# The planner of a 2-layer encoder kernel is given other durations for TensorE's products, and a price for each change of tile form

## The chip, the cores and the metric

One core of a Trainium2 chip. The metric is the device time of one launch in microseconds (us); lower is better. The kernel before took 1587.9 us (median of 3 runs, 1582.06 to 1589.01).

## The reference, cut to what matters

The kernel computes a small transformer-like trunk: one sequence of 256 tokens, width 1024, two layers, all in float32.

```python
for l in range(DEPTH):                       # 2
    h = modulate(rmsnorm(x, norm_gains[l, 0]), sh1, sc1)
    x = x + 0.5 * gt1 * swiglu(h, ffn_wi[l, 0], ffn_wo[l, 0])      # 1024 -> 2 x 2816 -> 1024
    h = modulate(rmsnorm(x, norm_gains[l, 1]), sh2, sc2)
    x = x + gt2 * hybrid_mixer(h, ...)
    h = modulate(rmsnorm(x, norm_gains[l, 2]), sh3, sc3)
    x = x + 0.5 * gt3 * swiglu(h, ffn_wi[l, 1], ffn_wo[l, 1])
return rmsnorm(x, final_norm)

# hybrid_mixer: proj = h @ w_in, then three token mixers of 8 heads x 64, then
merged = (sigmoid(gz0) * (o_a @ w_branch[0])      # a: dilated window attention
          + sigmoid(gz1) * (o_b @ w_branch[1])    # b: neighbourhood attention on a grid
          + sigmoid(gz2) * (o_c @ w_branch[2]))   # c: RWKV-7 recurrence, forward and backward
return merged @ w_out
```

The shifts, scales and gates (sh1, sc1, gt1 and so on) come from a conditioning vector through the weights `ada_w`.

## The kernel before, in words

**Dense work.** Activations lie transposed, features on the partitions and the 256 tokens along the free dimension. Every float32 weight tile is split in two parts, `whi` (ScalarE, line 352) and `wlo` (VectorE, line 361), each activation likewise, and one dense step is three matmuls of 128x128 by 256 (lines 395 to 398). Weights stream from HBM: SP issues a load of 512 KB (line 337), ScalarE and VectorE split it in quarters of 512 columns, and each quarter serves four dense steps. The product of the attention's v uses steps of three matmuls of 512 columns (lines 1645 to 1647). `pearly` are dense products that start before the norm is known.

**Mixer.** Its dense work is the stream of projections, gates and branch products in the order "cabAgB" (line 27): the recurrence's inputs first, then both attentions' inputs, then gates and branches a and b, and last the branch of the recurrence, whose input is `oC`. Beside it runs *thin* work: many small products on 64x64, 64x128, 128x64 or 128x32 parts of TensorE's array. The recurrence is computed in 4 chunks of 64 tokens in each of two directions. `invert` (line 1142) builds the chunk's matrix (pG), inverts its 8x8 blocks (p from m and b8), and doubles the block size three times (pX, pT); `values` prepares pBT, pvt, pMV; `scan` (line 1275) goes from chunk to chunk (pAS, pU, pS1, pY); `post` (line 1373) normalises the result (pvar, a square root, pgi) and writes `oC`. `attend` (line 1465) does the attentions (pS, pPT, po). Each of these steps has VectorE or ScalarE work between its products.

**The order.** Every engine runs its instructions in the order in which they were issued, and that order is made by a planner, `Order` (lines 58 to 155), when the program is built. The work is written as threads (generators). A thread asks for an engine and a duration with `on(engine, duration)` before it issues the instructions; `od.run` always lets that thread go on whose request can start earliest in planned time, and of several the one of the lowest priority number. The dense stream (`main`, line 1783) has priority 7, so thin work that is ready goes first; the splitting of weights has -1. A planned result can be used after a latency (line 36: 0.2 us after TensorE, 0.15 after ScalarE, 0.13 after VectorE). One rule speaks for the dense stream: thin work adds up in `thin`, and once that is over 2.25 us the dense stream goes first until it has had two steps in a row (lines 122 and 139 to 146). `clock` (line 103) slows planned products where TensorE has been little used. The planned durations decide the order and nothing else: no instruction waits for a planned time. The loads of `ada_w` are requested at planned times (`ada`, line 492: every 5 us in the first feed-forward part, every 7 us from 110 us after the start of the mixer).

A dense step is planned at `MM`, 0.329 us. A form of products (64x64 and so on) is not known to the planner before.

```python
36  LAT, MM = {"PE": 0.2, "ACT": 0.15, "DVE": 0.13, "SP": 0.0}, 0.329
...
139                 if a == "PE":
140                     if th is self.dense:
141                         self.row += 1
142                         if self.row >= BURST:
143                             self.thin = 0.0
144                     else:
145                         self.row = 0
146                         self.thin += b
147                     b = self.clock(t, b, 0.98 if th is self.dense else 0.6) - t
148                 self.free[a] = t + b
149                 th.t = t + b + lat
```

Of the kernel before, what the change touches and what calls it, by code (L numbers as in the profile page):

```python
# [34 lines left out]
WPRIO = -1  # L35
LAT, MM = {"PE": 0.2, "ACT": 0.15, "DVE": 0.13, "SP": 0.0}, 0.329
VPRIO = 4
# [20 lines left out]
class Order:  # L58
# [6 lines left out]
    def __init__(self):  # L65
        self.threads, self.free, self.cur, self.n = [], {}, None, 0
        self.dense, self.cols, self.thin, self.row, self.tab = None, {}, 0.0, 0, None

    def spawn(self, gen, prio, dense=False):
# [47 lines left out]
    def run(self):  # L117
        while self.threads:
# [11 lines left out]
            if kind == "on":  # L130
# [5 lines left out]
                if a == "ACT" and th.req[4] not in (None, self.tab):  # L136
                    self.tab = th.req[4]
                    b += 1.28
                if a == "PE":
                    if th is self.dense:  # L140
                        self.row += 1
                        if self.row >= BURST:
                            self.thin = 0.0
                    else:
                        self.row = 0
                        self.thin += b
                    b = self.clock(t, b, 0.98 if th is self.dense else 0.6) - t
# [10 lines left out]

def on(eng, dur, lat=None, tab=None):
    return ("on", eng, dur, LAT[eng if isinstance(eng, str) else eng[0]] if lat is None else lat, tab)  # L160

# [26 lines left out]
def trunk(ctx, tc, A, out):  # L188
# [404 lines left out]
    def rstd(st):  # L593
# [3 lines left out]
        p = paux("pss")  # L597
        yield on("PE", 0.6)
        for t in range(2):
# [268 lines left out]
    def mixer(l, st):  # L868
# [92 lines left out]
        def lowrank(d, q, tw, xl_, lw, pe):  # L961
# [37 lines left out]
            p = paux("pa", (128, 2, S))  # L999
            yield on("PE", 0.86)  # L1000
            for h in range(2):
# [12 lines left out]
        def kk_norm():  # L1014

            pss = None
            for d in range(2):
                yield wait(e_rkv[d, 1])
                yield take(s_big)
                kq = big("kq")  # L1020
                for hp in range(4):
                    yield on("ACT", 0.4)
                    S_.activation(kq[:, hp], RKV[d, 1][:, hp], AF.Square, scale=vec[:, 6, hp:hp + 1])
                if d == 0:
                    yield take(s_px)
                    pss = paux("pkk", (128, S))
                yield on("PE", 0.5)
                head_sum(pss, d, kq, d == 1)
                free_big()
# [17 lines left out]
        def finish():  # L1047
            pbs = None
            for d in range(2):
                yield wait(e_rkv[d, 0])  # L1050
                yield wait(e_kk)
                for q in range(2):
# [8 lines left out]
                    p = paux("pinv", (128, 2, S))  # L1061
                    yield on("PE", 0.434)
                    head_bcast(p, d, q, KK)
# [37 lines left out]
                if d == 0:  # L1101
                    yield take(s_px)
                    pbs = paux("pbs", (128, S))
                yield on("PE", 0.5)
                head_sum(pbs, d, RKV[d, 1], d == 1)
# [7 lines left out]
            for d in range(2):  # L1113
                yield wait(e_rkv[d, 2])
                v = RKV[d, 2]
                for q in range(2):
                    sl = slice(2 * q, 2 * q + 2)
                    yield take(s_px)
                    p = paux("pbon", (128, 2, S))
                    yield on("PE", 0.434)  # L1120
                    head_bcast(p, d, q, rows)
# [20 lines left out]
        def invert(d, cc):  # L1142
            for c in cc:
# [10 lines left out]
                for i in range(4):  # L1154
                    yield on("PE", 0.435, 0.2 if i == 3 else 0.0)
                    for b in range(2):
# [12 lines left out]
                for lv in range(3):  # L1169
                    by = lambda t: t.rearrange("p h (q a s) -> p h q a s", a=2, s=8 << lv)  # L1170
                    yield take(s_px)
                    px = paux("pX", (128, 4, 64))
                    yield on("PE", 0.615)
                    for h in range(8):
# [8 lines left out]
                    pt = paux("pT", (128, 4, 64))  # L1183
                    yield on("PE", 0.615)
                    for h in range(8):
# [54 lines left out]
        def values(d, c, G, bu, W1, cs_, done):  # L1240
            yield wait(e_rkv[d, 2])
            v = RKV[d, 2]
            for b in range(2):
                hs = half(b)
                yield take(s_px)
                p = paux("pBT", (128, 4, 64))
                yield on("PE", 0.22)
                for i in range(4):
# [5 lines left out]
            p = paux("pvt", (128, 4, 64))  # L1254
            yield on("PE", 0.648)
            for h in range(8):
# [6 lines left out]
            p = paux("pMV", (128, 4, 64))  # L1263
            yield on("PE", 0.615)
            for h in range(8):
# [9 lines left out]
        def scan(d):  # L1275
            ST = None
            order = list(range(4)) if d == 0 else [3, 2, 1, 0]
            for n, c in enumerate(order):
# [4 lines left out]
                if ST is not None:  # L1283
                    yield take(s_px)
                    p = paux("pAS", (128, 4, 64))
                    yield on("PE", 0.615)
                    for h in range(8):
# [5 lines left out]
                p = paux("pU", (128, 4, 64))  # L1293
                yield on("PE", 0.615)
                for h in range(8):
# [7 lines left out]
                if n < 3:  # L1303
                    yield take(s_px)
                    p = paux("pS1", (128, 4, 64))
                    yield on("PE", 0.615)
                    for h in range(8):
# [13 lines left out]
                p = paux("pY", (128, 4, 64))  # L1321
                yield on("PE", 1.275 if ST is not None else 0.615)
                for h in range(8):
# [49 lines left out]
        def post(d, t):  # L1373
# [13 lines left out]
            p = paux("pvar", (128, 8))  # L1387
            yield on("PE", 0.8)
            for hp in range(4):
# [75 lines left out]
        def attend(br, hps, qT, kT, vv, evs, o, pp, done):  # L1465
# [6 lines left out]
            for hp in hps:  # L1472
# [11 lines left out]
                pS = [paux("pS", (128, 2, S)) for _ in range(2)]  # L1484
                yield on("PE", 0.96)
                for t in range(2):
# [37 lines left out]
                po = paux("po", (128, S))  # L1524
                yield on("PE", 0.96)
                for j in range(2):
# [100 lines left out]
        def qkv(br):  # L1627
# [11 lines left out]
            for kk in range(KT):  # L1639
                yield from tl.whole()  # L1640
                wh, wl = tl.last
                for t in range(2):
                    xs = slice(t * 128, (t + 1) * 128)
                    yield on("PE", 0.65, 0.0)
                    P.matmul(p[t], ha.hi(kk)[:, xs], wh, start=kk == 0, stop=False)  # L1645
                    P.matmul(p[t], ha.hi(kk)[:, xs], wl, start=False, stop=False)
                    P.matmul(p[t], ha.lo(kk)[:, xs], wh, start=False, stop=kk == 7)  # L1647
# [260 lines left out]
```

## Time and profile before

| what | before |
|---|---|
| median of 3 runs | 1587.9 us |
| lowest, highest run | 1582.06, 1589.01 us |
| the profiled execution's own time | 1586.35 us |
| its span, first to last instruction | 1584.6 us |
| mean granted TensorE clock | 0.985 of full speed |
| TensorE busy | 1533.1 us, 97% |
| VectorE busy | 1311.7 us, 83% |
| ScalarE busy | 897.0 us, 57% |
| matmul records | 14518 |

The profile is of one execution. PE is TensorE, DVE VectorE, ACT ScalarE; PEclk is the clock that was granted to TensorE, as a share of full speed. The start of a matmul is measured and its end is modelled: matmuls overlap in the records, so the distance from one start to the next tells what one costs, and a busy engine can still have short waits in it. One float32 matmul of a thin product stands as two records, so a product of eight has 16.

### The profile page before, as it was taken

What the parts mean: (1) busy time and instruction counts of PE and PEld (TensorE: products, weight loads), DVE (VectorE), ACT (ScalarE), POOL (GpSimd) and SP (SyncE); (2) the same over time, 40 slices, a digit from 0 to 9 for tenths busy, and PEclk for the clock granted to TensorE, in tenths of its full rate; (3) what the DMA queues carried; (4) which work ended last, traced back from release to release, by engine and by line L of the source; (5) the groups of instructions that cost most, each with busy time, mean ns of one, the idle gap of its engine ahead of it and who ended that gap; (6) DMA issues with size and microseconds to landing.
All of it is one profiled execution on the core that took longest, in us unless ns stands there. A gap on an engine that the chain in (4) does not pass through costs nothing.

```text
span 1584.6 us, 36797 instructions
## 1 busy us (share of the span) xinstructions
PE 1533.1 (97%) x14518; PEld 1450.6 (92%) x14518; DVE 1311.7 (83%) x2938; ACT 897.0 (57%) x1854; POOL 21.3 (1%) x29
## 2 busy tenths in 40 slices
PE   3999999999999989999999999999999999999998
PEld 3999999988888889999999999998888987999997
DVE  7878889989888869997779877898888896888664
ACT  4655567576554447554565545676655445565554
POOL 3100000000000000000000000000000000000000
PEclk7999999999999989999999999999999999899999
DMA  8588864545464225888657876544446422467553
GB/s 310 188 293 272 284 230 163 180 130 198 140 230 140 74 80 174 277 287 273 226 200 272 285 266 203 185 159 155 160 159 232 168 102 68 136 202 274 184 184 127
DMA packets 91621, 311.61 MB, mean 197 GB/s; under 512 B 11444, under 2 KB 14772, under 8 KB 91448
## 3 DMA queue, kind: packets, MB, share of 16 engines
q1 hardware_dynamic: 91160, 309.15, 57.8%
q8 instruction: 114, 1.87, 0.5%
q14 instruction: 59, 0.48, 0.1%
q10 hardware_dynamic: 288, 0.10, 0.0%
HBM read 308.17 MB, written 1.05 MB: 195 GB/s over the span
## 4 chain that ended last, share of the span: by engine, by line
PE 88%; DMA 5%; DVE 4%; issue 1%; ACT 1%; SPq 0%; DVEq 0%; ACTq 0%
PE pmain L396 21%; PE pmain L397 20%; PE pmain L398 20%; DMA araw<-in_ada_w_dram 5%; PE pearly L396 2%; PE pearly L398 2%; PE pearly L397 2%; PE pX L1175 2%; PE pT L1186 2%; PE pG L1158 1%; PE pS L1488 1%; PE po L1528 1%; DVE wlo L361 1%; PE pmain L1645 1%; PE pmain L1647 1%
## 5 line engine op out<-in xcount | busy, mean ns | idle before, releaser
L352 ACT CAST whi<-wraw 128x512 fp32r<-128x512 f32 x836 | 511.9, 619 | 427.3 <-PE pmain L397 256.0
L361 DVE TENSOR_TENSOR wlo<-wraw,whi 128x512 fp32r<-128x512 f32 x836 | 571.7, 688 | 118.7 <-ACT whi L352 109.2
L396 PE MATMUL pmain<-h,whi 128*128 128x256 f32 x1872 | 539.2, 288 | 0.0
L398 PE MATMUL pmain<-h,wlo 128*128 128x256 f32 x1872 | 525.2, 281 | 1.1 <-DVE wlo L361 1.1
L397 PE MATMUL pmain<-h,whi 128*128 128x256 f32 x1872 | 525.2, 281 | 0.0
L396 PEld LDWEIGHTS pmain<-h,whi 128*128 128x128 f32 x1872 | 351.7, 188 | 13.3 <-issue 4.6
L398 PEld LDWEIGHTS pmain<-h,wlo 128*128 128x128 f32 x1872 | 352.2, 188 | 1.6 <-DVE wlo L361 1.6
L397 PEld LDWEIGHTS pmain<-h,whi 128*128 128x128 f32 x1872 | 352.3, 188 | 0.4
L460 DVE CUSTOM_DVE_ANT_0 araw<-araw,csb 128x1024 f32<-128x1024 f32 x137 | 169.0, 1235 | 47.6 <-DMA araw<-in_ada_w_dram 47.2
L398 PE MATMUL pmain<-z,wlo 128*128 128x256 f32 x704 | 198.2, 282 | 3.4 <-DVE wlo L361 3.3
L397 PE MATMUL pmain<-z,whi 128*128 128x256 f32 x704 | 197.9, 281 | 0.0
L396 PE MATMUL pmain<-z,whi 128*128 128x256 f32 x704 | 197.8, 281 | 0.0
L398 PEld LDWEIGHTS pmain<-z,wlo 128*128 128x128 f32 x704 | 132.6, 188 | 4.4 <-DVE wlo L361 4.2
L396 PEld LDWEIGHTS pmain<-z,whi 128*128 128x128 f32 x704 | 132.6, 188 | 0.0
L397 PEld LDWEIGHTS pmain<-z,whi 128*128 128x128 f32 x704 | 132.6, 188 | 0.0
L396 PE MATMUL pearly<-xh,whi 128*128 128x258 f32 x320 | 91.4, 286 | 0.0
L398 PE MATMUL pearly<-xh,wlo 128*128 128x258 f32 x320 | 90.4, 282 | 0.0
L397 PE MATMUL pearly<-xl,whi 128*128 128x258 f32 x320 | 90.2, 282 | 0.0
L397 PEld LDWEIGHTS pearly<-xl,whi 128*128 128x128 f32 x320 | 60.6, 189 | 0.0
L396 PEld LDWEIGHTS pearly<-xh,whi 128*128 128x128 f32 x320 | 60.4, 189 | 0.0
L398 PEld LDWEIGHTS pearly<-xh,wlo 128*128 128x128 f32 x320 | 60.3, 189 | 0.0
L419 ACT CAST z<-ffz 128x256 fp32r<-128x256 f32 x76 | 30.7, 405 | 40.3 <-DVE ffz L651 39.9
(306 smaller groups left out, 2459.2 us busy)
## 6 DMA issues: line engine op xcount, KB each, us to landing
wraw<-in_ffn_wi_dram SPq DMA_DIRECT2D x164, 512.0 KB, 4.9
araw<-in_ada_w_dram SPq DMA_DIRECT2D x137, 512.0 KB, 6.4
wraw<-in_ffn_wo_dram SPq DMA_DIRECT2D x88, 512.0 KB, 4.5
wraw<-in_w_in_dram SPq DMA_DIRECT2D x78, 512.0 KB, 3.7
wraw<-in_w_gb_dram SPq DMA_DIRECT2D x72, 512.0 KB, 4.2
wraw<-in_w_out_dram SPq DMA_DIRECT2D x16, 512.0 KB, 3.6
w0raw<-in_ffn_wi_dram SPq DMA_DIRECT2D x12, 512.0 KB, 9.8
raw<-in_ada_w_dram SPq DMA_DIRECT2D x7, 512.0 KB, 7.9
```

Source lines behind the costliest of these rows:

```text
L352: S_.copy(hi, part(q))
L361: V.tensor_tensor(lo, part(q), hi, op=OP.subtract)
L396: P.matmul(o, w[0], xh, start=first, stop=False)
L397: P.matmul(o, w[0], xl, start=False, stop=False)
L398: P.matmul(o, w[1], xh, start=False, stop=last)
L419: S_.copy(self.hi(k), src)
L460: V.tensor_tensor_reduce(out=raw, in0=raw, in1=csb, scale=0.5, scalar=0.0, op0=OP.mult, op1=OP.add, accum_out=modT[l][:, blk:blk + 1])
L1158: P.matmul(pp[b][:, i], BK[d][i // 2][hs, i % 2, c].rearrange("p a b -> p (a b)"), ar_view(d, i // 2)[hs, :, i % 2, cs_], start=True, stop ...
L1175: P.matmul(px[half(h), h // 2], G[half(h), h // 2, h % 2, 0:64], T[half(h), h // 2], start=True, stop=True)
L1186: P.matmul(pt[half(h), h // 2], X[half(h), h // 2], TT[half(h), h // 2], start=True, stop=True)
L1488: P.matmul(pS[e][:, t], qT[half(e), hp, t * 128:(t + 1) * 128], kT[half(e), hp], start=True, stop=True)
L1528: P.matmul(po[half(e)], vv[:, j, (2 * hp + e) * 64:(2 * hp + e + 1) * 64], pt_[:, 2 * e + j], start=j == 0, stop=j == 1)
```

## The change

No instruction is added or removed. The planner gets other durations for TensorE's requests: a dense step 0.354 (was 0.329), a step of the v product 0.7 (0.65), eight 64x64 products 0.48 (0.615), each of the four requests of pG 0.22 (0.435), and so on. Each request on TensorE can now name its form; one that names none is of the full array (or of the 65 rows of pwz). Where the form differs from that of the request planned before it on TensorE, 0.2 us (`TURN`) is added, and this sum also goes into `thin`. All other code is as before. The sites that are alike stand once, with their number.

```diff
-LAT, MM = {"PE": 0.2, "ACT": 0.15, "DVE": 0.13, "SP": 0.0}, 0.329
+LAT, MM = {"PE": 0.2, "ACT": 0.15, "DVE": 0.13, "SP": 0.0}, 0.354
+TURN = 0.2
...
+        self.form = None
...
                 if a == "PE":
+                    if th.req[5] != self.form:
+                        self.form = th.req[5]
+                        b += TURN
                     if th is self.dense:
...
-def on(eng, dur, lat=None, tab=None):
-    return ("on", eng, dur, LAT[eng if isinstance(eng, str) else eng[0]] if lat is None else lat, tab)
+def on(eng, dur, lat=None, tab=None, form=None):
+
+    return ("on", eng, dur, LAT[eng if isinstance(eng, str) else eng[0]] if lat is None else lat, tab, form)
...
         p = paux("pss")
-        yield on("PE", 0.6)
+        yield on("PE", 0.9)
...
             p = paux("pa", (128, 2, S))
-            yield on("PE", 0.86)
+            yield on("PE", 0.86, form="64x128")
...
                     pss = paux("pkk", (128, S))
-                yield on("PE", 0.5)
+                yield on("PE", 0.44, form="128x32")
...
                     p = paux("pinv", (128, 2, S))
-                    yield on("PE", 0.434)
+                    yield on("PE", 0.48, form="64x128")
...
                 for i in range(4):
-                    yield on("PE", 0.435, 0.2 if i == 3 else 0.0)
+                    yield on("PE", 0.22, 0.2 if i == 3 else 0.0, form="64x128")
...
                     px = paux("pX", (128, 4, 64))
-                    yield on("PE", 0.615)
+                    yield on("PE", 0.48, form="64x64")
...
                 p = paux("pBT", (128, 4, 64))
-                yield on("PE", 0.22)
+                yield on("PE", 0.25, form="64x128")
...
                     p = paux("pS1", (128, 4, 64))
-                    yield on("PE", 0.615)
+                    yield on("PE", 0.48, form="128x64")
...
                 p = paux("pY", (128, 4, 64))
-                yield on("PE", 1.275 if ST is not None else 0.615)
+                yield on("PE", 1.05 if ST is not None else 0.48, form="128x64")
...
             p = paux("pvar", (128, 8))
-            yield on("PE", 0.8)
+            yield on("PE", 0.9)
...
                 pS = [paux("pS", (128, 2, S)) for _ in range(2)]
-                yield on("PE", 0.96)
+                yield on("PE", 0.87, form="64x128")
...
                 po = paux("po", (128, S))
-                yield on("PE", 0.96)
+                yield on("PE", 0.87, form="128x64")
...
                 for t in range(2):
                     xs = slice(t * 128, (t + 1) * 128)
-                    yield on("PE", 0.65, 0.0)
+                    yield on("PE", 0.7, 0.0)
```

pX's edit stands for pT, pMV, pAS and pU (0.615 to 0.48) and pvt (0.648 to 0.48), all of form 64x64; pkk's for pbs; pinv's for pbon. pwz, pcum, pPT, p, pg and pgi keep their durations and name no form.

## Rows read from the trace of the kernel before

**Rows 1.** The page: busy time of the engines, and the chain by engine.

```profile
PE 1533.1 (97%) x14518; PEld 1450.6 (92%) x14518; DVE 1311.7 (83%) x2938; ACT 897.0 (57%) x1854; POOL 21.3 (1%) x29
...
PE 88%; DMA 5%; DVE 4%; issue 1%; ACT 1%; SPq 0%; DVEq 0%; ACTq 0%
```

**Rows 2.** Stretches: length, busy us and count of each engine, granted clock, DMA.

```profile
core 0: us, PE busy (x) PEld busy (x) DVE busy (x) ACT busy (x) POOL busy (x), PEclk, DMA share, GB/s
100.00:200.00 100.00, 98.86 (x833) 98.31 (x832) 84.99 (x170) 53.53 (x104) 1.07 (x9) 1.00 0.84 286
600.00:700.00 100.00, 100.00 (x851) 100.00 (x850) 91.24 (x196) 62.16 (x124) 0.00 (x0) 1.00 0.72 247
...
300.00:569.00 269.00, 266.23 (x3111) 230.68 (x3109) 229.19 (x601) 147.65 (x345) 0.00 (x0) 1.00 0.45 149
1072.00:1341.00 269.00, 266.28 (x3111) 230.79 (x3109) 229.09 (x602) 147.71 (x344) 0.00 (x0) 1.00 0.44 149
...
500.00:569.00 69.00, 68.93 (x1160) 59.63 (x1154) 54.69 (x160) 31.18 (x66) 0.00 (x0) 1.00 0.23 78
569.00:577.60 8.60, 3.78 (x45) 2.95 (x44) 5.04 (x12) 4.63 (x10) 0.00 (x0) 0.78 0.19 61
577.60:584.20 6.60, 6.56 (x28) 6.14 (x29) 3.78 (x9) 2.03 (x4) 0.00 (x0) 0.51 0.00 0
...
1349.30:1355.80 6.50, 6.40 (x28) 5.97 (x29) 3.62 (x9) 1.91 (x5) 0.00 (x0) 0.53 0.00 0
```

**Rows 3.** Timeline of VectorE at 602 us: a wlo and its successor.

```profile
602.24 0.69 DVE L361 TENSOR_TENSOR wlo<-wraw,whi 128x512 fp32r<-128x512 f32 x1
602.84 0.48 DVE L535 SCALAR_TENSOR_TENSOR xl<-xT,Ac,xh 128x256 fp32r<-128x256 f32 x1
```

**Rows 4.** Timeline of TensorE, 551.8 to 556 us: start, duration, what.

```profile
551.80 0.68 PE L1288 MATMUL pAS<-ST,ar 64*64 64x64 f32 x16
552.41 0.39 PE L396 MATMUL pmain<-o,whi 128*128 128x256 f32 x1
...
552.96 0.68 PE L1175 MATMUL pX<-txw,G 64*64 64x64 f32 x16
553.58 0.46 PE L1249 MATMUL pBT<-c_ident,bk 64*128 64x64 f32 x4
553.97 0.68 PE L1296 MATMUL pU<-txw 64*64 64x64 f32 x16
554.48 0.63 PE L1186 MATMUL pT<-txw 64*64 64x64 f32 x16
555.04 0.39 PE L396 MATMUL pmain<-o,whi 128*128 128x256 f32 x1
...
555.95 0.45 PE L1324 MATMUL pY<-G,bu 128*64 128x64 f32 x8
```

**Rows 5.** Timeline of TensorE: the first change of form in layer 0.

```profile
261.97 1.03 PE L972 MATMUL pwz<-lw,xlow 65*128 65x256 f32 x4
```

**Rows 6.** Timeline of TensorE, 568.8 to 578 us.

```profile
568.79 0.28 PE L398 MATMUL pmain<-o,wlo 128*128 128x256 f32 x1
569.00 0.33 PE L1324 MATMUL pY<-G,bu 128*64 128x64 f32 x2
570.05 0.68 PE L1324 MATMUL pY<-G,bu 128*64 128x64 f32 x14 [0.72 <-ACT bu L1300]
...
572.47 1.05 PE L1390 MATMUL pvar<-c_sel,gsq 128*128 128x2 f32 x8 [1.13 <-ACT gsq L1382]
575.12 1.11 PE L1408 MATMUL pgi<-c_ident,gsq 128*128 128x128 f32 x4 [1.59 <-DVE gsq L1403]
577.64 0.58 PE L396 MATMUL pmain<-oC,whi 128*128 128x256 f32 x1 [1.41 <-ACT oC L1435]
```

**Rows 7.** Stretches, with line 396 alone: its count is that of dense steps.

```profile
300.00:450.00 150.00, 58.37 (x196) 36.86 (x196) 1.00 0.52 172
450.00:500.00 50.00, 20.98 (x67) 12.57 (x67) 1.00 0.52 180
500.00:569.00 69.00, 18.93 (x57) 10.69 (x57) 1.00 0.23 78
```

**Rows 8.** Waits of TensorE: for whom, us in total, times, longest.

```profile
PE pmain L398 <- DVE wlo L361: 4.4, 5, 1.6
...
PE p L1222 <- DVE m L1217: 3.7, 4, 1.0
...
PE pX L1175 <- DVE txw L1238: 1.4, 2, 0.8
```

More of the change, by code (lines that the diff above doesn't have):

```diff
@@ L1103, in finish @@
                     pbs = paux("pbs", (128, S))
-                yield on("PE", 0.5)
+                yield on("PE", 0.44, form="128x32")
                 head_sum(pbs, d, RKV[d, 1], d == 1)
@@ L1119, in finish @@
                     p = paux("pbon", (128, 2, S))
-                    yield on("PE", 0.434)
+                    yield on("PE", 0.48, form="64x128")
                     head_bcast(p, d, q, rows)
@@ L1183, in invert @@
                     pt = paux("pT", (128, 4, 64))
-                    yield on("PE", 0.615)
+                    yield on("PE", 0.48, form="64x64")
                     for h in range(8):
@@ L1254, in values @@
             p = paux("pvt", (128, 4, 64))
-            yield on("PE", 0.648)
+            yield on("PE", 0.48, form="64x64")
             for h in range(8):
@@ L1263, in values @@
             p = paux("pMV", (128, 4, 64))
-            yield on("PE", 0.615)
+            yield on("PE", 0.48, form="64x64")
             for h in range(8):
@@ L1285, in scan @@
                     p = paux("pAS", (128, 4, 64))
-                    yield on("PE", 0.615)
+                    yield on("PE", 0.48, form="64x64")
                     for h in range(8):
@@ L1293, in scan @@
                 p = paux("pU", (128, 4, 64))
-                yield on("PE", 0.615)
+                yield on("PE", 0.48, form="64x64")
                 for h in range(8):
@@ L1305, in scan @@
                     p = paux("pS1", (128, 4, 64))
-                    yield on("PE", 0.615)
+                    yield on("PE", 0.48, form="128x64")
                     for h in range(8):
```

## The prediction, made before the change was run

> **What bounds the kernel now.** I read the page's busy times first, then its chain, then stretches, then the waits. TensorE is busy 97% of the span, and the chain that ends last runs through it for 88% [rows 1]. So time is what TensorE does, plus the few places where it stands still or runs at the lower clock. The stretches show where those are [rows 2]. In the dense stage from 600 to 700 us it is busy 100.00 of 100 us at a granted clock of 1.00, the 2.4 GHz level. In the mixer's two stretches of mixed work, 300 to 569 and 1072 to 1341 us, it is busy 266.2 and 266.3 of 269. Right behind each comes a hole: 3.78 us busy of 8.60, then a stretch at 0.51 of the clock, the 1.2 GHz level with an edge at each end; layer 1 repeats it. The chip granted less after TensorE had been mostly idle.
>
> The change alters no instruction, only the order in which a planner written in Python issues them. So three things can move: the holes, the number of times TensorE changes its tile form, and the stalls of an engine that meets an instruction too early. The profiled execution took 1586.35 us for a span of 1584.6; the median of the three runs is 1587.9, 1.5 us above it, which I treat as nothing.
>
> **How wrong the plan is before.** VectorE's costs in the plan are right: a wlo starts 0.60 us before its successor [rows 3] and is planned at 0.6. TensorE's are too low. From 600 to 700 us 851 dense products run, 283.7 steps of three; planned at 0.329 that is 93.3 us of the 100, at 0.354 it is 100.4 [rows 2]. In mixed work I take one piece, from the pAS at 551.80 to the pY at 555.95, 4.15 us [rows 4]. Before: 0.615 (pAS) + 0.329 + 0.615 (pX) + 0.22 (pBT) + 0.615 (pU) + 0.615 (pT) + 2 x 0.329 = 3.67. After, with 0.2 at each change of form: 0.68 + 0.554 + 0.68 + 0.45 + 0.68 + 0.48 + 0.908 = 4.43. So the plan goes from 12% fast to 7% slow here. The same reckoning over all 3111 products from 300 to 569 us [rows 2] gives 242.6 us before and 275.8 after, against 269.
>
> **What a change of form costs.** A thin product and one dense step, 551.80 to 552.96, take 1.16 us [rows 4]; the plan's own 0.48 and 0.354 leave 0.33 for two changes, about 0.16 each. There are 223 a layer, from the pwz at 261.97 [rows 5] to the pvar at 572.47 [rows 6], 446 in all and some 70 us. A visit to dense work in between costs two, 0.32 us.
>
> **The sum, part by part.** The work itself: same products, 0.
>
> The holes. In layer 0 the last dense product before the hole starts at 568.79 and oC's first one at 577.64 [rows 6]: the chain of the last chunk (pY, ACT's square, pvar, a square root, pgi, VectorE's products, the cast of oC) is run with nothing beside it. TensorE's stands in 569.0 to 577.6 are 8.60 - 3.78 = 4.8 us, and by pitch rather than by modelled ends some 5.9 (8.7 us less pY 1.2, pvar 1.0, pgi 0.6). Then 577.6 to 584.2 holds 28 products, 6.6 us at half clock, worth 3.3 [rows 2]. Together 9.1 us a layer, 18.2 for both. What would fill it is dense work left over when the recurrence ends. Why more is left: the recurrence waits on VectorE and ScalarE, whose planned times stay; a dense step now fills 0.354 of such a wait and not 0.329, and 0.554 where it follows a thin product. Bounds: from 300 to 569 us there are 196 + 67 + 57 = 320 dense steps [rows 7]. Replaying the planner's rule for bursts (lines 139 to 147) over that order, 54 of them are forced by the sum of thin work; the other 266 fill waits (the v product's steps are left aside). At least 0.025/0.354 = 7% of these, 19 steps or 6.7 us, come free if the waits set the pace, and none if thin work does. At most, if the recurrence took its old 242.6 planned us, 1 - 242.6/275.8 = 12% of 269, 32 us, come free. I take the lower figure that has waits in it, 6.7 us: over the 5.9 idle, and with the idle gone I let the stretch at half clock go too. So -18.2, between 0 and -18.2, since no hole is left after that.
>
> The stalls. Before, the plan was 10% fast on TensorE, so operands were there when it came. That slack goes. Its idle time in mixed work is now 269 - 266.2 and 269 - 266.3, 5.5 us in both layers [rows 2]; most of it is p behind m, 3.7, and pX, 1.4 [rows 8]. I let it double, as the smallest step that a lost slack of 10% suggests: +5.5, between 0 and +13.6 (worked out with the second rival).
>
> The other edits. pG's four planned steps of 0.435 become four of 0.22, so fewer bursts cut it up and a few changes of form may go. pss, pvar, pkk, pbs, pinv and pbon occur at most 8 times a layer. The v product's 0.70 for 0.65 follows the same ratio as the dense step. All 0, covered by the chain of waits around them, at worst a microsecond or two.
>
> The loads of the modulation weights are issued at planned times (every 5 or 7 us); with a plan no longer 10% fast they come some 8 to 10% closer in real time, on SP's queue ahead of weight loads. DMA is at a share of 0.84 from 100 to 200 us [rows 2], and TensorE's waits for wlo are 4.4 us in all [rows 8]. Between 0 and another 4.4; I take +1, nearer to nothing, since those waits are five in some 1000 us of dense work.
>
> Sum: 1586.35 - 18.2 + 5.5 + 1 = 1574.7, so **1575**.
>
> **Rivals.** First, thin work sets the pace and the holes stay. In the last 69 us 26 of 57 dense steps [rows 7] are forced, and the budget that forces them fills as before: thin work planned at 44.8 us then is 35.4 plus 48 entries of 0.2, 45.0. For it: TensorE is at 68.93 of 69 there [rows 2]. Against: before 500 us only 28 steps are forced, against the 196 + 67 that run there [rows 7], and the recurrence is on its way from some 360 us on. Time 1586.
>
> Second, slower: the stalls. A change is priced 0.2 and costs 0.16, so the plan is now slow in mixed work, 275.8 against 269. Products are put where the plan has their operands ready, and TensorE, in order, gets there early. It can lose at most what the plan is too slow, 6.8 us a layer, 13.6 in all; it decides if most of the 85 dense visits a layer end at an operand that comes within the 0.08 us (two changes of 0.04) by which a visit is over-priced. Holes unfilled: 1586.4 + 13.6 = 1600, half of it 1593. Against: VectorE is busy 229 of 269 us [rows 2], and has queued work rather than late work.
>
> Third, more changes of form. A visit of two steps can become one of one step, since one now fills 0.554 planned us. If 44 such visits are added, 44 x 0.32 = 14 us, 1600 with the holes as they are. The Trainium skill (TensorEngine Tiling, Key Properties) says that a change of tiling mode drains the engine, so that their number counts and not only their length; the 0.16 us here agrees.
>
> Fourth, the other way: chains ripen together during longer planned visits, and a tenth to a fifth of the 446 changes go, 7 to 14 us at 0.16. Beside filled holes: 1561 to 1568, about 1565.
>
> **How the numbers follow.** Forecast 0.45, holes stay 0.22, stalls 0.13, more changes 0.05, fewer changes 0.15. Faster or slower begins at 0.5%, 8 us (under 1580, over 1596), about what a measurement can tell. Faster: most of the forecast, 0.38, and 0.14 of the last, 0.52. Slower: 0.17 from stalls, more changes and holes that stay with new stalls. Same: 0.31. The range reaches from the fourth rival nearly in full, 1562, to the second and third nearly in full, 1598.
>
> **What would show it.** Dense products beside the last pY, pvar and pgi of each layer, and a granted clock of 1.00 through that stretch; if pgi still has an idle microsecond ahead of it, the filling was wrong. Changes of form near 446; p, pX or pY with more idle time before them than now would show the stalls. The dense stages should keep their length. I would be wrong if the mixed stretch itself grew while the holes closed: then work only moved.

## The result: slower by 1.4%, though the holes closed

The changed kernel takes 1607.88 us, the median of four runs from 1602.44 to 1612.11. Before it was 1584.98, the median of four. The ratio is 1.0142, with a 95% interval of 1.0114 to 1.0171. The forecast was 1575 with a range up to 1598, so the result lies outside on the slow side. The profiled execution of after took 1610.05 us for a span of 1607.9, that of before 1586.35 for 1584.6: +23.3 us of span to explain. In after the lines of the kernel file that are named here have a number higher by 6 (L361 is L367, L460 is L466).

The page of after, busy time and chain by engine, to be held against [rows 1], with one group of VectorE's instructions, its reductions:

```profile
PE 1539.5 (96%) x14518; PEld 1453.3 (90%) x14518; DVE 1315.4 (82%) x2963; ACT 893.6 (56%) x1833; POOL 21.5 (1%) x29
...
PE 71%; DVE 14%; DMA 10%; issue 3%; ACT 1%; SPq 0%; DVEq 0%; ACTq 0%
...
L466 DVE CUSTOM_DVE_ANT_0 araw<-araw,csb 128x1024 f32<-128x1024 f32 x137 | 169.0, 1235 | 74.9 <-DMA araw<-in_ada_w_dram 74.8
```

The same 14518 products run, but the chain now leaves TensorE for 29% of the span where it left it for 12%: VectorE went from 4% to 14%, DMA from 5% to 10%. The last line says what they do there. L466 is the reduction that VectorE makes of each block of modulation weights, `araw`. It idled 74.8 us ahead of these for their DMA, 46 times; before it was 47.2 us, 39 times. The waits of VectorE (for whom, us in total, times, longest), before:

```profile
DVE araw L460 <- DMA araw<-in_ada_w_dram: 47.2, 39, 3.2
```

After:

```profile
DVE araw L466 <- DMA araw<-in_ada_w_dram: 74.8, 46, 4.7
```

Then the stretches of after, columns as in [rows 2]: one whole stage of up products in layer 0 (the second feed-forward), the last 9.20 us ahead of oC's products in layer 0, where the hole was, and one piece inside that up stage.

```profile
core 0: us, PE busy (x) PEld busy (x) DVE busy (x) ACT busy (x) POOL busy (x), PEclk, DMA share, GB/s
643.43:754.75 111.32, 106.84 (x866) 105.82 (x865) 92.26 (x185) 55.66 (x111) 0.00 (x0) 0.97 0.79 269
576.00:585.20 9.20, 9.20 (x82) 9.20 (x81) 7.13 (x14) 5.16 (x11) 0.00 (x0) 1.00 0.67 209
743.60:747.00 3.40, 3.40 (x17) 3.40 (x17) 3.37 (x7) 0.93 (x2) 0.00 (x0) 0.50 0.66 187
```

And the same up stage before:

```profile
639.02:740.53 101.51, 101.51 (x866) 101.51 (x865) 90.49 (x185) 55.30 (x111) 0.00 (x0) 1.00 0.82 284
```

The hole is gone: where [rows 2] had 3.78 us busy of 8.60 and then a stretch at 0.51 of the clock, TensorE is now busy 9.20 of 9.20 us at 1.00; over the whole chain from the last pY to oC, 565.00 to 585.22, it is busy 20.22 of 20.22. But a stage with the same 866 products takes 111.32 us for 101.51, with 4.5 us of idle time and a mean clock of 0.97. Seventeen products fill 3.40 us at a clock of 0.50, the 1.2 GHz level, in the middle of dense work.

Cut at the first product of each stage, TensorE's timeline gives the whole account:

| stretch, us | before | after | |
|---|---|---|---|
| seven feed-forward stages with modulation loads | 590.4 | 614.9 | +24.5 |
| mixed stage, layer 0 / 1 | 329.1 / 329.1 | 328.9 / 334.5 | +5.3 |
| oC stage behind it, layer 0 / 1 | 14.8 / 14.5 | 11.3 / 11.4 | -6.6 |
| all other | 306.7 | 306.9 | +0.2 |

Of the 24.5, stops account for 16.6 by TensorE's pitch: 20 gaps of over 0.3 us between two products' starts, 22.1 us beyond the usual 0.118, where before there were 6 with 5.5. The lower clock accounts for 5.1, half of 10.2 us in three stretches. The remaining 2.8 is pitch, the distance from one start to the next where nothing stops.

Last, TensorE's waits in after, against [rows 8] (for whom, us in total, times, longest):

```profile
PE pmain L404 <- DVE wlo L367: 18.7, 17, 2.0
...
PE p L1228 <- DVE m L1223: 6.4, 11, 1.5
...
PE pX L1181 <- DVE txw L1244: 5.3, 12, 1.2
```

The wait for `wlo`, 4.4 us before, is 18.7: a product waits for the low half of a weight that VectorE has not split yet. VectorE's busy time has not grown (1311.7 to 1315.4). So VectorE has the time, and does the split late.

**One stop, followed.** Timelines of after show why (start, duration, what, and in brackets the idle time ahead of it with what ended that). SP's queue:

```profile
732.11 2.31 SPq L343 DMA_DIRECT2D wraw<-in_ffn_wi_dram  x2
734.47 0.44 SPq L493 DMA_DIRECT2D araw<-in_ada_w_dram  x1
```

VectorE in the same stretch:

```profile
733.37 0.69 DVE L367 TENSOR_TENSOR wlo<-wraw,whi 128x512 fp32r<-128x512 f32 x1
734.91 1.22 DVE L466 CUSTOM_DVE_ANT_0 araw<-araw,csb 128x1024 f32<-128x1024 f32 x1 [0.85 <-DMA araw<-in_ada_w_dram]
736.07 0.08 DVE L466 DVE_READ_ACCUMULATOR2_ANT modT<- 128x1 f32 x1
736.07 1.29 DVE L367 TENSOR_TENSOR wlo<-wraw,whi 128x512 fp32r<-128x512 f32 x2
...
738.06 0.68 DVE L367 TENSOR_TENSOR wlo<-wraw,whi 128x512 fp32r<-128x512 f32 x1
738.66 0.42 DVE L427 TENSOR_TENSOR z<-ffz,z 128x256 fp32r<-128x256 f32 x1
741.49 1.23 DVE L466 CUSTOM_DVE_ANT_0 araw<-araw,csb 128x1024 f32<-128x1024 f32 x1 [2.41 <-DMA araw<-in_ada_w_dram]
...
742.64 1.89 DVE L367 TENSOR_TENSOR wlo<-wraw,whi 128x512 fp32r<-128x512 f32 x3
```

ScalarE, the casts that make the high halves for the three splits at 742.64:

```profile
738.49 0.62 ACT L358 CAST whi<-wraw 128x512 fp32r<-128x512 f32 x1
740.33 1.14 ACT L358 CAST whi<-wraw 128x512 fp32r<-128x512 f32 x2 [1.22 <-DMA wraw<-in_ffn_wi_dram]
```

TensorE around its stop:

```profile
741.12 0.28 PE L403 MATMUL pmain<-h,whi 128*128 128x256 f32 x1
743.38 0.42 PE L404 MATMUL pmain<-h,wlo 128*128 128x256 f32 x1 [1.98 <-DVE wlo L367]
```

The split that starts at 733.37 frees a buffer of raw weights. SP, which stood at a load for that buffer, issues it and right behind it the load of an `araw` block, at 734.47. VectorE makes three more splits (two at 736.07, one at 738.06) and then meets the reduction of that block. Its data are not there: VectorE stands for 2.41 us until 741.49, seven microseconds after the issue. Three splits stand behind it. The first has had its high half since 739.11 and could have run at once; the other two have theirs by 741.5. TensorE needs the first, and stops after the product at 741.12 until that split is done. The stretch at a clock of 0.50 begins 0.2 us after TensorE resumes.

The Trainium skill (Perfetto Trace Analysis, Tensor Engine Instruction) says that VectorE, ScalarE and GpSimd take their instructions strictly first in, first out, while TensorE may pull a weight load ahead; the trace agrees, since the three splits start only at 742.64, behind the reduction.

The plan counts on less. In `ada_load` SP's slot is 1.45 us and `od.set(got, 2.0)` lets the block land 2.0 us later, 3.45 in all. Part 6 of the page gives the median from issue to landing (columns: count, KB each, us). Before:

```profile
araw<-in_ada_w_dram SPq DMA_DIRECT2D x137, 512.0 KB, 6.4
```

After:

```profile
araw<-in_ada_w_dram SPq DMA_DIRECT2D x137, 512.0 KB, 6.1
```

### The profile page after: what moved, and what is told of

Same layout as the page of the kernel before. It is cut to its first block, busy times and chain, and to the rows that moved or that the text cites. A ratio compares the mean times of both kernels' runs of the same rounds, so it can differ in the third digit from the quotient of the medians.

```text
span 1607.9 us, 36801 instructions
## 1 busy us (share of the span) xinstructions
PE 1539.5 (96%) x14518; PEld 1453.3 (90%) x14518; DVE 1315.4 (82%) x2963; ACT 893.6 (56%) x1833; POOL 21.5 (1%) x29
## 4 chain that ended last, share of the span: by engine, by line
PE 71%; DVE 14%; DMA 10%; issue 3%; ACT 1%; SPq 0%; DVEq 0%; ACTq 0%
PE pmain L402 17%; PE pmain L404 16%; PE pmain L403 16%; DMA araw<-in_ada_w_dram 8%; DVE wlo L367 4%; PE pearly L402 2%; PE pearly L404 2%; PE pearly L403 2%; DVE araw L466 2%; DVE G L1169 1%; PE pX L1181 1%; PE pT L1192 1%; PE pmain L1651 1%; PE pfirst L403 1%; PE pPT L1525 1%
## 5 line engine op out<-in xcount | busy, mean ns | idle before, releaser
L367 DVE TENSOR_TENSOR wlo<-wraw,whi 128x512 fp32r<-128x512 f32 x836 | 570.1, 687 | 119.3 <-ACT whi L358 113.1
L466 DVE CUSTOM_DVE_ANT_0 araw<-araw,csb 128x1024 f32<-128x1024 f32 x137 | 169.0, 1235 | 74.9 <-DMA araw<-in_ada_w_dram 74.8
## 6 DMA issues: line engine op xcount, KB each, us to landing
raw<-in_ada_w_dram SPq DMA_DIRECT2D x7, 512.0 KB, 10.5
```

What stands on the lines that cost most here:

```text
L367: V.tensor_tensor(lo, part(q), hi, op=OP.subtract)
L466: V.tensor_tensor_reduce(out=raw, in0=raw, in1=csb, scale=0.5, scalar=0.0, op0=OP.mult, op1=OP.add, accum_out=modT[l][:, blk:blk + 1])
```

## The experiments

Three theories stood at the start. **Landing**: the plan's landing time for these blocks is too early, and the slower pace of planned TensorE had no slack left to hide it. **Pace**: the loads come closer in real time, as the plan is no longer 10% fast, and crowd the weight loads; this is the term of the prediction that was priced at 1 us. **Over-priced change**: the second rival, 0.2 us for a change of form that costs 0.16. All medians below stand against runs of the kernel before on the same chip, 1583.3 to 1584.0 us. "Dense" is the sum of the seven feed-forward stages of the table above (590.4 before, 614.9 after), "mixed" that of both mixed and both oC stages (687.4 and 686.2).

**The pace stretched back** by 7.6%:

```diff
-PACE, START = 7, 110
-FPACE, FSTART = 5, 12
+PACE, START = 7.53, 118
+FPACE, FSTART = 5.38, 13
```

> The changed kernel, with the planned times of the modulation weights' loads stretched by 0.354/0.329 (5 to 5.38 us, 7 to 7.53). Theory PACE (loads come closer in real time and crowd out the dense weights): the up-projection stages return from 98.0, 111.3 and 108.3 us to 92 to 103, TensorE's waits for wlo fall from 18.7 us to some 5, total 1583 to 1592. Theory LANDING (VectorE stands in line behind a reduction whose load is planned to land too early): hardly a change, waits for wlo above 12 us, total 1600 to 1610.

Measured: 1594.35 us, 1.0072 [1.0047, 1.0096]. Neither theory's number. Its waits (VectorE's for the blocks, TensorE's for the splits):

```profile
DVE araw L466 <- DMA araw<-in_ada_w_dram: 71.2, 47, 4.4
...
PE pmain L404 <- DVE wlo L367: 14.5, 17, 3.4
```

Both stay nearer to after's 74.8 and 18.7 than to before's 47.2 and 4.4. Dense is 609.7, so it got back 5 of the 24.5. Another 11 us came out of the mixed stages (675.4, the shortest of all the kernels here), where nothing of the kind was expected.

**The landing corrected**, one number in `ada_load`:

```diff
-        od.set(got, 2.0)
+        od.set(got, 5.0)
```

> The changed kernel, with the landing of a modulation weight block planned 5 us after its issue slot and not 2. Theory LANDING: VectorE's waits for these blocks fall from 74.8 us to below 40, TensorE's waits for wlo from 18.7 to some 5, total 1583 to 1592. Theory PACE: the DMA engines are as crowded as before, waits for wlo above 12 us, total 1600 to 1610.

Measured: 1582.35 us, 0.9995 [0.9982, 1.0007]. All of the loss is gone, to within what can be told from no change. VectorE's waits:

```profile
DVE wlo L367 <- ACT whi L358: 148.2, 235, 3.5
...
DVE bt L1487 <- DMA bt<-in_bt_dram: 7.8, 2, 3.9
...
DVE araw L466 <- DMA araw<-in_ada_w_dram: 0.9, 1, 0.9
```

The wait for the blocks fell from 74.8 to 0.9 us, TensorE has no wait for `wlo` left in the dense stages, and dense is 586.2. VectorE now waits for the high halves, 148.2 us, which costs nothing: it is ahead of TensorE. In each of the two long up stages (the second feed-forward of layer 0, the first of layer 1) 20 of these loads are issued, as in after and against 18 before. They follow each other at 4.96 us in the mean, closer than in after (5.37 and 5.31), and yet no up stage is more than 1.6 us longer than before. That settles landing against pace. One wait grew, from 4.4 us in after to 7.8: the load of `bt`, the attention's bias, has the same mistake in the plan (0.6 + 2.2 us planned, 4.1 by the page).

**The dense step's duration back, the changes of form kept:**

```diff
-LAT, MM = {"PE": 0.2, "ACT": 0.15, "DVE": 0.13, "SP": 0.0}, 0.354
+LAT, MM = {"PE": 0.2, "ACT": 0.15, "DVE": 0.13, "SP": 0.0}, 0.329
...
-                    yield on("PE", 0.7, 0.0)
+                    yield on("PE", 0.65, 0.0)
```

> The changed kernel, with the dense step planned at 0.329 and the v step at 0.65 again; forms, their price and the thin durations stay. If the dense step's 0.354 costs the time (PACE or LANDING): dense stages as in the kernel before (within 2 us each), total 1580 to 1590. If the price of a change and the thin durations cost it: mixed stages as slow as after (from first mixed dense product to oC 329 and 334 us), total above 1600.

Measured: 1590.49 us, 1.0054 [1.0027, 1.008]. Dense is 593.0, near before's 590.4, and the waits too:

```profile
DVE araw L466 <- DMA araw<-in_ada_w_dram: 47.0, 39, 3.4
...
PE pmain L404 <- DVE wlo L367: 4.8, 7, 1.3
```

The holes are filled all the same (oC stages 11.45 and 11.31), and the changes of form fell from 446 to 418. Between the profiled executions it lost 3.6 us of span against before: 2.6 in the dense stages and 2.1 in the mixed ones (689.5, though the holes are filled; there `p` waits 9.3 us and `pX` 6.4), with 1.0 won elsewhere. Its median lies just above the 1580 to 1590 that were expected.

**The dense step's duration alone** (the kernel before with 0.354 and 0.7, nothing else):

```diff
-LAT, MM = {"PE": 0.2, "ACT": 0.15, "DVE": 0.13, "SP": 0.0}, 0.329
+LAT, MM = {"PE": 0.2, "ACT": 0.15, "DVE": 0.13, "SP": 0.0}, 0.354
...
-                    yield on("PE", 0.65, 0.0)
+                    yield on("PE", 0.7, 0.0)
```

> The kernel before, with the dense step planned at 0.354 and the v step at 0.7, nothing else changed. If the dense step's duration costs the time: up-projection stages about 98, 111 and 108 us as after, total 1600 or more. If it is the forms: total 1575 to 1590.

Measured: 1605.55 us, 1.0145 [1.0118, 1.0172], the loss of the whole change. Waits:

```profile
DVE araw L460 <- DMA araw<-in_ada_w_dram: 62.3, 48, 3.5
...
PE pmain L398 <- DVE wlo L361: 16.9, 19, 1.9
```

Dense is 605.2; mixed is 690.3, with the holes filled or nearly so (oC 11.31 and 12.92). So the loss in the dense stages comes with the 0.354, 14.8 us of the 24.5, and either half of the change fills the holes by itself. The stops are those of after, 22 gaps with 20.7 us against 20 with 22.1; what is missing is after's stretches at the lower clock (5.1 us) and its longer pitch, and two of the three up stages are shorter than after's 111.3 and 108.3 (table below).

**The landing corrected in the kernel before:**

```diff
-        od.set(got, 2.0)
+        od.set(got, 5.0)
```

> The kernel before, with the landing of a modulation weight block planned at 5 us and not 2, nothing else. Theory LANDING with slack: the plan that is 10% fast on TensorE already covers late blocks in the dense stages, so VectorE's waits for them go (47 to below 10 us) and the time stays within 4 us of before, 1579 to 1587. Rival (a late landing always costs): 1570 or less.

Measured: 1602.12 us, 1.0117 [1.0103, 1.013]. A miss. The dense stages did as forecast, 585.5. But mixed grew to 705.7. The one longest stop there, on TensorE's timeline:

```profile
1219.26 1.12 PE L1175 MATMUL pX<-txw,G 64*64 64x64 f32 x16 [4.80 <-DVE txw L1238]
```

No DMA stands behind this one. The blocks' reductions lie elsewhere in the plan, VectorE's order in the mixed stage is another, and here a transpose came 4.80 us late; 12.6 and 21.5 us of the two layers ran at the lower clock. Over the kernels here the mixed stages take from 675.4 to 705.7 us, 12 less to 18 more than before, for small changes of the plan, and the totals of single kernels can't be read without taking the stages apart.

**Landing and pace together:**

```diff
-PACE, START = 7, 110
-FPACE, FSTART = 5, 12
+PACE, START = 7.53, 118
+FPACE, FSTART = 5.38, 13
...
-        od.set(got, 2.0)
+        od.set(got, 5.0)
```

> The changed kernel with the landing at 5 us and the loads' pace stretched too (5.38, 7.53 us). If crowding of loads still costs after the landing is right: 2 to 8 us less than with the landing alone, 1575 to 1580. If only the landing mattered: within 3 us of it, 1579 to 1586.

Measured: 1585.09 us, 1.0009 [1.0, 1.0019]; dense 586.7, mixed 688.5. With the landing right, the pace does nothing in the dense stages.

**Landing, and a change priced at what it costs:**

```diff
-TURN = 0.2
+TURN = 0.16
...
-        od.set(got, 2.0)
+        od.set(got, 5.0)
```

> The changed kernel with the landing at 5 us and a change of form priced at 0.16 us, as the trace shows it, and not 0.2. If the over-priced change makes TensorE wait in mixed stages: their idle time falls from 6.8 and 6.0 us, total 3 to 8 us less than with the landing alone. If not: within 3 us of it, 1579 to 1586, either way.

Measured: 1581.27 us, 0.999 [0.9978, 1.0003]; mixed 685.2 against 682.1 with 0.2. TensorE's idle time in the mixed stages is 6.1 and 10.7 us, against 6.8 and 6.0: one layer hardly less, one more, and in layer 0 a hole is back (its oC stage takes 15.63 us). That gives no sign that the price of a change makes the stalls.

**Landing, and the bias load of the attention:**

```diff
-                        yield on("SP", 0.6, 2.2)
+                        yield on("SP", 0.6, 5.0)
```

> The changed kernel with the landing at 5 us, and the loads of the second attention's bias tile planned to land 5 us after their slot and not 2.2. Theory LANDING, the same in another place: VectorE's wait of 3.84 us for the bias tile and TensorE's 3 us for pU behind it go in both layers, with the stretch at half clock after each: 6 to 12 us less than with the landing alone, 1570 to 1577. If that wait is hidden elsewhere: within 3 us of it.

Measured: 1575.66 us, 0.9949 [0.9937, 0.9962], runs from 1574.62 to 1576.7. The wait for `bt` fell from 7.8 to 1.9 us and TensorE's wait at `pU` behind it, 6.0, went. Yet mixed is 682.1, the same as without it: others took its place.

```profile
PE pX L1181 <- DVE txw L1244: 9.6, 9, 2.2
PE p L1228 <- DVE m L1223: 7.1, 14, 1.1
```

So the total lies in the range that was expected, but not by the way expected: the gain of 7 us in the median over the version with the landing alone isn't explained by this wait. In the profiled executions the spans differ by 5.4 us, and 4.0 of these lie in the dense stages (582.2), where one up stage ran at a median pitch of 114 ns and not 118. All five runs here are under all ten of the version with the landing alone (1580.25 to 1585.43), so the gain is real; whether the shorter pitch belongs to the order or to that one execution, and so where the gain comes from, stays open.

**Where is the edge?** If each reduction that comes sooner costs in proportion, the kernel before with an earlier landing should lose too. The slack that after lost was, by the plan's own numbers, about 0.25 us:

```diff
-        od.set(got, 2.0)
+        od.set(got, 1.75)
```

> The kernel before, with the landing of a modulation weight block planned at 1.75 us and not 2: in real time that is about the 0.25 us by which the change moved each reduction nearer to its load (3.45 planned us are 3.71 real ones at the old pace and 3.45 at the new). Theory LANDING: VectorE waits more for these blocks (47 us towards 75), TensorE for wlo (4.4 towards 15 or more), the dense stages grow by 10 to 25 us in sum, total 1590 to 1610. Rival (the exact plan of TensorE takes away the slack in some other way, the landing only hides it): dense stages within 4 us of before, total 1578 to 1590.

Measured: 1590.9 us, 1.004 [1.0026, 1.0054]. A miss: dense is 588.4, no longer than before, and the reductions wait no more than before:

```profile
DVE araw L460 <- DMA araw<-in_ada_w_dram: 45.2, 42, 3.4
```

So the loss is no smooth function of the planned landing. What differs is a whole number. I counted, for each block, the splits in VectorE's order between the one that frees the raw buffer (and so lets SP come to the block's load) and the block's reduction. Reductions with three or fewer, in the up stages of layer 0 (first and second feed-forward) and of layer 1 (first), beside the length of those stages in us:

| kernel | three or fewer | lengths |
|---|---|---|
| before | 0 / 0 / 0 | 92.1 / 101.5 / 102.2 |
| before, landing 1.75 | 0 / 0 / 0 | 91.4 / 102.0 / 101.8 |
| 0.329 back | 0 / 0 / 0 | 91.8 / 102.5 / 102.3 |
| pace stretched | 0 / 4 / 4 | 92.2 / 106.8 / 107.3 |
| 0.354 alone | 3 / 4 / 4 | 98.9 / 106.2 / 103.9 |
| after | 3 / 4 / 4 | 98.0 / 111.3 / 108.3 |
| after, landing 3.5 (below) | 0 / 0 / 0 | 91.1 / 102.2 / 102.2 |
| after, landing 5.0 | 0 / 0 / 0 | 91.0 / 103.1 / 102.7 |

In all eight kernels one of these stages is longer exactly where three or four reductions stand behind only three splits, by 1.2 us at the least against the longest of the same stage without any. A single one gives no clear sign: the second feed-forward's up stage of layer 1 has one in after, 0.354 alone and pace stretched, and takes 103.1, 101.4 and 104.1 us, against 102.3 before with none. This fits the landing measured: an up stage of 101.51 us holds 72 splits, 1.41 us each, and 6.1 to 6.4 us are 4.3 to 4.5 of these. Behind four splits, 5.6 us, the block is nearly there; behind three, 4.2 us, it is some 2 us off. These are estimates from medians. The waits bear them out: in after's feed-forward stages the 16 reductions behind three splits waited 1.80 us in the mean, the 27 behind four 1.02, those behind five or more not at all. TensorE feels the step more sharply, since its weights are split some way ahead: of the 22.1 us of its stops, 14.7 come right after one of the 16, 4.8 after one of the 27, and 2.6 after another wait of VectorE, 2.84 us for the load of the positions (`posb`); before, 40 reductions stood behind four, and the stops after them were 1.8 us. In the plan 3.45 us are 2.6 splits of four steps at 0.329, and 2.4 at 0.354, so the reduction could go one place further forward.

**Half of the correction**, to see whether the place alone decides:

```diff
-        od.set(got, 2.0)
+        od.set(got, 3.5)
```

> The changed kernel with the landing planned at 3.5 us, half the way to 5. Theory LANDING: VectorE's waits for the blocks between 74.8 and 0.9 us, some 15 to 30, TensorE's waits for wlo below 6 us, dense stages within 6 us in sum of those with 5 us. Rival (it is the other order of the whole that helps, not the wait): no such step in between, dense stages anywhere.

Measured: 1596.27 us, 1.0087 [1.0063, 1.011]. In the dense stages the length is as foreseen, 587.9; the waits for the blocks, 6.0 us in all, are below the 15 to 30 expected, since all but five of the blocks in the feed-forward stages stand behind five splits or more. The total is higher because mixed is 699.6; there TensorE waits

```profile
PE p L1228 <- DVE m L1223: 15.8, 9, 6.5
```

for `m`, which a product of VectorE makes: again another order in the mixed stages, and again not the dense ones.

**Two versions built on the result.** Both correct the landing and the `bt` load. The first also plans the pair of VectorE's operations ahead of `p` (L1218) longer:

```diff
-        od.set(got, 2.0)
+        od.set(got, 5.0)
...
-            yield on("DVE", 0.42)
+            yield on("DVE", 0.65)
...
-                        yield on("SP", 0.6, 2.2)
+                        yield on("SP", 0.6, 5.0)
```

> The changed kernel with the landing at 5 us, the bias tile's at 5 us, and the two VectorE steps ahead of m planned at 0.65 us and not 0.42 (the reduction alone takes more than 0.6). If p's waits for m come from that: they fall from 7.1 us to below 3 and the total by 2 to 5 us against the run without it, 1571 to 1574. If the order of the mixed stages is luck: those stages move by up to 6 us either way, 1568 to 1583.

Measured: 1574.11 us, 0.994 [0.9926, 0.9955]: faster than both kernels, 0.6% under before and 34 us under after, but only some 1.5 us under the version without the 0.65, where 2 to 5 were expected; their intervals overlap. TensorE's waits:

```profile
PE pX L1181 <- DVE txw L1244: 7.6, 13, 1.2
```

The wait at `p` fell from 7.1 to 1.1 us and that at `pX` from 9.6 to 7.6; dense is 584.1, mixed 680.3. Not all is well in it: layer 0's oC stage is at 15.19 us again, as before the change.

The second has the cheaper change of form in place of the 0.65:

```diff
-TURN = 0.2
+TURN = 0.16
...
-        od.set(got, 2.0)
+        od.set(got, 5.0)
...
-                        yield on("SP", 0.6, 2.2)
+                        yield on("SP", 0.6, 5.0)
```

> The changed kernel with the landing and the bias tile at 5 us and the change of form at 0.16 us. If the over-priced change causes waits in mixed stages: idle time there falls below 8 us a layer from 10.5 and 9.6, total 1569 to 1574. If the order of the mixed stages is luck: 1568 to 1583 and no clear sign, and the dense stages stay as they are.

Measured: 1576.82 us, 0.9956 [0.9938, 0.9973]; dense 585.0, mixed 680.2. TensorE's idle time in the mixed stages fell from 10.5 and 9.6 us to 5.7 and 8.9, of which only the first is below the 8 expected, and the total is 1.2 us more and not less. So the price of a change of form makes no difference to the time here either.

## Why the prediction was wrong

**The step that failed** is "The loads of the modulation weights". It saw the right object, and that its queue would shift; it bounded the cost by TensorE's waits for `wlo`, "between 0 and another 4.4", and took +1. The measured term is +24.5 us in the dense stages, of which 21.7 are stops and half clock. Two things were wrong in it. The mechanism: it looked at DMA (loads closer together on SP's queue), and the runs show that they may come closer still without loss (after with landing 5.0, 586.2 us). The place is VectorE's order: an instruction that waits for a DMA holds up all splits behind it. And the bound: a wait of 4.4 us on TensorE was taken as a measure of what could come. The measure that mattered was one view on, VectorE's own waits: 47.2 us for `araw` were there in the trace of before, with the landing at 6.4 us by the page against 3.45 in the code. They cost little then, since four splits of lead nearly covered them. A wait that is covered by a margin of one instruction is not a wait that costs nothing. The profiled execution missed the sum, 1574.7, by 35.4 us: 23.5 are this term, 11.6 the mixed stages below.

**"The dense stages should keep their length"** was wrong with it. The argument was that planned time there is now right; it was only one engine's planned time, and with TensorE planned 7% too quick (0.329 for 0.354) the plan put every other thing late by as much, measured in TensorE's work. That margin hid a wrong landing, as the run with 0.354 alone shows. It isn't a matter of the 0.25 us alone: taken off the landing in the kernel before, they cost nothing in the dense stages (588.4), because no more reductions came to stand behind three splits.

**The holes** were right: they closed in both layers, by dense work beside the last pY, pvar and pgi. The two oC stages lost 6.6 us, as the 3.3 each for the lower clock had it, and TensorE is busy throughout the place of [rows 6], with no idle time ahead of pvar and pgi:

```profile
567.46 1.05 PE L1396 MATMUL pvar<-c_sel,gsq 128*128 128x2 f32 x8
571.63 0.60 PE L1414 MATMUL pgi<-c_ident,gsq 128*128 128x128 f32 x4
```

That more dense work is left over was right too, and it didn't need the whole change: either half does it, so the 0.354 that the prediction gave as its reason suffices but isn't needed. Nor is it certain: in two corrected versions with the whole change the oC stage of layer 0 is back at 15.63 and 15.19 us.

**The stalls** were sized too low. The forecast for the mixed stages was 2 x 5.9 us off and 5.5 on; they came out 5.3 longer. If the 11.8 of the holes' idle time were won as forecast, 17 were taken back, over the upper bound of 13.6. Idle time that TensorE shows in them, without the hole, went from 5.6 to 18.9 us, and 3.4 us of layer 1 ran at half clock. Part of it is the same cause: VectorE's waits for blocks in the two mixed stages grew from 3.9 and 3.9 to 8.7 and 9.7. One case in full, VectorE's timeline of after:

```profile
1258.41 1.23 DVE L466 CUSTOM_DVE_ANT_0 araw<-araw,csb 128x1024 f32<-128x1024 f32 x1 [2.42 <-DMA araw<-in_ada_w_dram]
...
1260.16 0.16 DVE L1234 TENSOR_TENSOR w<-p,w 128x8 f32<-128x8 f32 x1
...
1261.70 0.45 DVE L1244 STREAM_TRANSPOSE txw<-txw 128x256 f32<-128x256 f32 x1
```

And TensorE's:

```profile
1262.20 0.98 PE L1181 MATMUL pX<-txw,G 64*64 64x64 f32 x16 [2.54 <-DVE w L1234]
```

The chain of small operations on `w` stands behind the reduction, and TensorE idles 2.54 us ahead of `pX`. The rest is put down to the other order itself. That is only a description: where the time goes can be read (the mixed stages have 12.3 us of idle time and no lower clock in the kernel with 675.4, 24.5 us and 34.1 us at the lower clock in the one with 705.7), but why one order stops TensorE more than another was not settled. The rival that named over-pricing as the cause of stalls isn't supported: 0.16 in place of 0.2 changed the total by less than 0.1% in both pairs. As the order alone moves these stages by more than 10 us, an effect of a few us can't be excluded.

**The changes of form** came out at 452, against "near 446", so the rivals with more or fewer of them were both out, and the 0 for the other edits isn't contradicted.

**The chances.** A slower kernel had 0.17, and its stated ways (stalls from over-pricing, more changes) were not the way that the 24.5 us went. What the list of rivals lacked was one that asked which planned numbers besides TensorE's are wrong. The plan's numbers had been held against the trace for `wlo` [rows 3] and for products [rows 4], and not for a single DMA. "VectorE's costs in the plan are right" rests on one split, too: of the two steps ahead of `m` that are planned at 0.42 us together, the reduction alone takes 0.63 in the mean of 16 before.

## What to carry to other kernels

A plan with several wrong durations can be in balance; here correcting one of them used up the slack that hid another, so hold every planned number against the trace, landings of DMAs first, and correct those that wait together. On an engine that works in order, look for instructions that wait for a DMA and count what stands between the issue and them: in after TensorE lost 0.2 us for each reduction behind four splits and 0.9 for each behind three. Judge such a change stage by stage, since here a total hid the closed holes behind a loss of 24 us elsewhere, and moved by 10 and more for reasons that stayed open.

## What the runs showed of the hardware

A load of an `araw` block, 512 KB on SP's queue, took 6.4 us before and 6.1 after in the median from its issue to its landing, beside the weight loads, at a DMA share of 0.82 and 0.79 in the up stages shown; in the twelve other versions it was 5.6 to 6.2. The weight loads `wraw` of the same size on the same queue took 3.6 to 4.9 us; the slowest of them, before:

```profile
wraw<-in_ffn_wi_dram SPq DMA_DIRECT2D x164, 512.0 KB, 4.9
```

The plan has 1.45 + 2.0 = 3.45 us for these too, which no run here corrected. The Trainium skill (DMA: Bandwidth & Descriptors, Anatomy of one DMA) has a fit of 2.0 us plus the bytes at 436 GB/s for loads that GpSimd issues; by it 512 KB would be an estimated 3.2 us, close to the plan's 3.45. The measured median is nearly twice that for `araw` and above it for the weights, and the measurement decides for loads among others.

The granted clock fell to 0.50, for 3.4 us each time, in otherwise full work of TensorE after single stops: in after behind stops of 1.81, 1.98, 2.02 and 2.54 us (the products at 699.09, 743.38, 961.98 and 1262.20). A stop of 1.83 us at 160.90 had no such stretch behind it, nor had any of the 22 stops in the dense stages with 0.354 alone, up to 1.9 us long, so the length of a stop alone does not foretell it. By an estimate, half of 3.4, each stretch costs about 1.7 us beyond the stop itself.
